# Expert weights by chunk, a hinted branch and an earlier read of z in a two-layer MoE backbone

## The chip, the cores and the metric

The kernel runs on one core of a Trainium2 chip. The metric is the device time of one execution in microseconds; each kernel is run several times, and the median is given. A trace of one more execution comes from the hardware profiler. Engines are named as the profile names them: PE (TensorE), PEld (its weight loads), DVE (VectorE), ACT (ScalarE), POOL (GpSimd) and SP (SyncE, which here only issues DMAs). A trailing q (PEq, SPq) is an engine's sequencer.

## What is computed

Two layers work on 256 latent and 256 context tokens of width 1024, all float32. Layer 0 has an even mixer (a short gated convolution beside differential attention), layer 1 an odd one (a bidirectional gated linear recurrence, RG-LRU). Each layer ends in a mixture of 16 experts, in 4 groups of 4; each token picks its best group and the two best experts in it. The change concerns these two mixtures:

```python
def hier_moe(h, w_grp, b_grp, w_rt, b_rt, w_gate, w_up, w_down):
    ...
    top_v, top_i = lax.top_k(e_sel, TOP_K)
    w_sel = jax.nn.softmax(top_v, axis=-1) * p_sel
    eid = g_idx[..., None] * EXPERTS_PER_GROUP + top_i
    gate = jnp.sum(jax.nn.one_hot(eid, N_EXPERTS, dtype=f32) * w_sel[..., None], axis=-2)
    hg = jnp.einsum('bsd,edf->bsef', h, w_gate)
    hu = jnp.einsum('bsd,edf->bsef', h, w_up)
    act = jax.nn.silu(hg) * hu * gate[..., None].astype(h.dtype)
    return jnp.einsum('bsef,efd->bsd', act, w_down)
```

`w_gate` and `w_up` are 1024x512 for each expert, `w_down` is 512x1024. Layer 0 works on all 512 tokens, layer 1 on the 256 latent ones.

## The kernel before

**Routed rows in slots.** Each expert has a fixed number of slots: `CAP0` = 96 (three row groups of 32, `NR`) in layer 0, `CAP1` = 64 (two, `NR1`) in layer 1. The experts are worked in four groups q = 0 to 3 of four. `four` (L1059) computes one product for the four experts at once: expert j's 32 rows stand as weights in a strip of 32 columns of the array (`tile_position=(0, 32*j)`), its 512 weight columns stream, and the sum over the contraction runs over chunks of 128: 8 for `wg` and `wu`, 4 for each half of `wd`. One *set* is one chunk of one row group: four products, which the trace shows as eight matmul instructions (float32 goes in two passes) and eight weight loads.

**Weights.** They come in tiles of 128x2048 (1 MB) into a pool of 23 units (`unit`, L94), reused in the order in which they come free. `load_ahead` (L118) issues the next loads of the list `todo` on SP while a unit is free and the number loaded ahead is under a limit; `wtile` takes the next tile, `used` gives it back. A tile of `wg` or `wu` holds one expert's four chunks, so `four` takes four tiles, uses them for all row groups and then frees the four together:

```python
for k0 in range(0, nk, 4):
    ws = [get(j, k0) for j in range(4)]
    for r in range(nr):
        for k in range(4):
            for j in range(4):
                T.matmul(...)
        between(r)
    used(*ws)
```

**A group.** `moe0` (L1082) and `moe1` (L1270) do, for each q: `wg` products, `silu` on ACT, `wu` products, `act` on DVE, the transposes of `act` (`transposed_act`, L1073), then the `wd` products of both halves of the output. In layer 0 the outputs of the first three groups go with indirect DMAs on POOL (`scatter`) to a DRAM tile `z` that has one row for each of a token's two choices; rows of the last group, and of tokens over capacity, are zeroed there by scatters of a zero tile. In layer 1 the outputs are summed on PE by a selection matrix `own` (L1326) into four banks that are held to the end.

**The branch.** A count of spilled rounds, `n`, is read by every engine. `spill_rounds` (L970) opens `tc.If(n > 0)` (L977) around a body for rows over capacity. With these inputs n is 0 in both layers, so the body is jumped over. It stands between the last transposes of group q = 3 and that group's `wd` products. Behind layer 0's branch SP issues the gates, four reads of `z` (1 MB each, `zb`), the first tile of the odd mixer's input projection, and then layer 1's modulation weights (`ada`). POOL sums and gates `zb` (L1221, L1222), DVE builds `own` (L1219) and later adds `zb` to `x` (L1249). In layer 1 half of the last group's `wd` loads stand behind the branch, because four tiles at a time come free.

**The order of work** is set by the order of the code on each engine's queue; every SP load waits for its unit and, at a branch, SP waits until the loads that it has issued have landed.

## Time and profile before

| | before |
|---|---|
| median of 3 runs, us | 1024.35 (1023.33 to 1025.01) |
| the profiled execution, us | 1023.78 |
| its span, us | 1022.0 |
| granted clock of TensorE, mean | 0.969 |
| PE, PEld, DVE, ACT, POOL busy | 93%, 51%, 42%, 28%, 13% |
| read from HBM | 303.23 MB |

Times in the trace count from the start of the span. A row of a timeline gives the start, the duration, the engine, the source line, the operation, the tile written and the tiles read, the number of instructions drawn together, and in brackets the idle time before it with what ended it. Layer 0's mixture of experts lies at about 325 to 619 us, layer 1's at about 788 to 1018 us. [...]

### The profile page before, as it was taken

The numbers are of one execution on the slowest core, as the hardware profiler recorded it, in microseconds if no ns is written. First come the engines' busy times: TensorE is split into PE (matmuls) and PEld (weight loads), VectorE is DVE, ScalarE is ACT, GpSimd is POOL, SyncE is SP. The second block draws the span as 40 slices with busy tenths as digits, with TensorE's granted clock in tenths as the row PEclk, the third lists the DMA queues.
The fourth block names the chain that finished last, engine by engine and source line by source line (L and its number), as shares of the span: only waits on it lengthen the run. The fifth ranks groups of instructions, "written<-read, shape, count | busy, mean of one in ns | idle before, by whom it ended". The sixth has DMA issues, their size and how long they took to land. (4 is left out here: it accounts for less than half of the span.)

```text
span 1022.0 us, 16136 instructions
## 1 busy us (share of the span) xinstructions
PE 946.8 (93%) x6705; PEld 516.2 (51%) x6705; DVE 424.2 (42%) x929; ACT 285.0 (28%) x503; POOL 137.7 (13%) x116
## 2 busy tenths in 40 slices
PE   4699999999995999999999799998986999999997
PEld 2488757656885343343433245787634443434333
DVE  3756766567465020020110157858866221212103
ACT  3623333324031110010110025669873110101000
POOL 0254010031033011011010161130410000000000
PEclk9799999999995999999999899999998999999999
DMA  8932466879667799999999787406585499999995
GB/s 363 381 110 114 165 211 252 323 267 420 262 211 274 294 391 404 421 410 416 421 361 422 260 319 284 165 1 211 181 321 214 165 421 420 421 420 420 422 382 203
DMA packets 49201, 309.68 MB, mean 303 GB/s; under 512 B 7432, under 2 KB 8200, under 8 KB 14560
## 3 DMA queue, kind: packets, MB, share of 16 engines
q1 hardware_dynamic: 45296, 300.58, 74.0%
q0 software_dynamic: 3824, 7.99, 2.1%
q8 instruction: 55, 0.90, 0.4%
q14 instruction: 26, 0.21, 0.1%
HBM read 303.23 MB, written 9.50 MB: 306 GB/s over the span
## 5 line engine op out<-in xcount | busy, mean ns | idle before, releaser
L1067 PE MATMUL ba<-w,hgT 128*32 128x512 f32 x1536 | 179.8, 593 | 1.0 <-DMA w<-in_wu_dram 0.9
L1067 PEld LDWEIGHTS ba<-w,hgT 128*32 128x32 f32 x1536 | 54.3, 110 | 114.1 <-issue 110.0
L1067 PE MATMUL ba<-w,actT 128*32 128x512 f32 x800 | 95.2, 593 | 1.9 <-DVEq L977 1.1
L178 PE MATMUL bz<-hT,wsp 128*128 128x256 f32 (+1 forms) x224 | 77.0, 345 | 0.3 <-ACT hT L155 0.3
L180 PE MATMUL bz<-hT,wsp 128*128 128x256 f32 (+1 forms) x224 | 74.2, 333 | 0.0
L179 PE MATMUL bz<-hT,wsp 128*128 128x256 f32 (+1 forms) x224 | 74.1, 332 | 0.0
L1067 PE MATMUL bz<-w,actT 128*32 128x512 f32 x480 | 56.7, 612 | 7.1 <-PEq L977 7.1
L1067 PEld LDWEIGHTS ba<-w,actT 128*32 128x32 f32 x800 | 33.4, 110 | 56.4 <-issue 49.7
L1067 PE MATMUL bz<-w,hgT 128*32 128x512 f32 x512 | 58.0, 592 | 0.0
L155 ACT ACTIVATE wsp<-w 128x512 fp32r<-128x512 f32 (+1 forms) x60 | 42.7, 765 | 50.0 <-PE bz L180 18.0
L158 DVE TENSOR_TENSOR wsp<-w,wsp 128x512 fp32r<-128x512 f32 (+1 forms) x49 | 48.2, 1013 | 10.2 <-ACT wsp L155 10.2
L178 PEld LDWEIGHTS bz<-hT,wsp 128*128 128x128 f32 x224 | 42.3, 189 | 7.3 <-ACT wsp L155 2.8
L180 PEld LDWEIGHTS bz<-hT,wsp 128*128 128x128 f32 x224 | 42.1, 189 | 4.8 <-issue 0.8
L179 PEld LDWEIGHTS bz<-hT,wsp 128*128 128x128 f32 x224 | 42.3, 189 | 4.3 <-DVE hT L158 0.8
L388 PE MATMUL bz<-w,sT 128*32 128x512 f32 x320 | 38.2, 595 | 4.3 <-DMA w<-in_ada_w_dram 4.3
L179 PE MATMUL bz<-wsp,hT 128*128 128x512 f32 x96 | 39.0, 406 | 3.4 <-DVE wsp L158 3.4
L178 PE MATMUL bz<-wsp,hT 128*128 128x512 f32 x96 | 38.5, 408 | 2.4 <-ACT hT L155 2.4
L1067 PEld LDWEIGHTS bz<-w,actT 128*32 128x32 f32 x480 | 16.6, 113 | 43.7 <-issue 43.7
L180 PE MATMUL bz<-wsp,hT 128*128 128x512 f32 x96 | 38.6, 403 | 0.0
L1452 DVE SCALAR_TENSOR_TENSOR uc<-bz,ocw,uc 128x510 f32<-128x510 f32 (+2 forms) x48 | 35.1, 744 | 8.3 <-ACT uc L1450 7.6
L1467 POOL TENSOR_TENSOR uc<-uc,ii 128x512 f32<-128x512 f32 x16 | 25.8, 1621 | 92.7 <-ACT ii L1421 92.6
L1191 DVE SCALAR_TENSOR_TENSOR act<-ba,tg,silu 128x512 f32<-128x512 f32 x6 | 4.5, 751 | 78.4 <-PE ba L1067 78.4
(374 smaller groups left out, 1465.6 us busy)
## 6 DMA issues: line engine op xcount, KB each, us to landing
w<-in_wg_dram SPq DMA_DIRECT2D x64, 1024.0 KB, 12.3
w<-in_wu_dram SPq DMA_DIRECT2D x64, 1024.0 KB, 12.7
w<-in_wd_dram SPq DMA_DIRECT2D x64, 1024.0 KB, 12.2
w<-in_ada_w_dram SPq DMA_DIRECT2D x48, 1024.0 KB, 8.2
w<-in_od_w_in_dram SPq DMA_DIRECT2D x8, 1024.0 KB, 8.4
w<-in_w_qkv_dram SPq DMA_DIRECT2D x6, 1024.0 KB, 9.2
w<-in_w_conv_dram SPq DMA_DIRECT2D x6, 1024.0 KB, 5.0
w<-in_ev_w_out_dram SPq DMA_DIRECT2D x4, 1024.0 KB, 9.4
```

Source lines behind the costliest of these rows:

```text
L155: S.activation(hi, src, AF.Copy)
L158: (eng or lo_engine()).tensor_sub(lo, src, hi.bitcast(F))
L178: T.matmul(o, l[0], r[0], start=start, stop=False)
L179: T.matmul(o, l[0], r[1], start=False, stop=False)
L180: final[0] = T.matmul(o, l[1], r[0], start=False, stop=stop)
L388: T.matmul(m[32 * j:32 * j + 32], sT[:, k], w[:, j * 512:(j + 1) * 512], start=(k == 0), stop=(k == KD - 1), tile_position=(0, 32 * j))
L1067: T.matmul(o[r][32 * j:32 * j + 32], rows(r, k0 + k)[:, 32 * j:32 * j + 32], ws[j][:, k], start=(k0 + k == 0), stop=(k0 + k == nk - 1), ti ...
L1191: V.scalar_tensor_tensor(act[r], u[r], tg[:, n:n + 1], sl[r], op0=ALU.mult, op1=ALU.mult)
L1452: V.scalar_tensor_tensor(c[:, :, j:256], src[:, :, 0:256 - j], tap, c[:, :, j:256], op0=ALU.mult, op1=ALU.add)
L1467: G.tensor_mul(uc[:, n], uc[:, n], ii)
```

## The change

- **Weights by chunk.** The host lays the expert weights out so that a 1 MB tile holds one chunk of all four experts of a group (`fours`, `w_group`). `four` goes through the chunks one by one, all row groups for each, and frees a tile after its chunk. With `last=4` (the `wu` of layer 0, and both halves of `wd` of its last group) the last four chunks are taken together, row group by row group, as before.
- **A hint for the branch.** `spill_hint(l)` marks, on all five engines, the usual outcome of the branch ahead of the `wu` products of q = 3. The barrier-free form of the branch is asked for.
- **z is cleared once,** in the even mixer: a memset on POOL and four DMAs of 1 MB on SP. The scatters of zeros are gone.
- **z is read ahead of the branch** in layer 0: gates, the four reads, POOL's sums and the first projection tile. DVE's `own` stays behind the branch. The units come from the last `wu` tiles.
- **Layer 1's gates** are read ahead of the branch, and all eight `wd` loads of the last group now stand ahead of it.
- The body of the branch works its 16 experts as four loops of four, so that its code is about four times as long. It is not entered here.

```diff
-    def w_first(l, es):
+    def w_group(l, q):
+
         for n in ("wg", "wu"):
-            for k0 in (0, 4):
-                todo.extend(((n, l, e, k0), [128, 4, 512], a[n][l, e][:, k0:k0 + 4]) for e in es)
-
-    def w_second(l, es):
+            todo.extend(((n, l, q, k), [128, 4, 512], a[n][l, q][:, k]) for k in range(KD))
         for h in range(2):
-            todo.extend((("wd", l, e, h), [128, 4, 512], a["wd"][l, e, h]) for e in es)
+            todo.extend((("wd", l, q, h, k), [128, 4, 512], a["wd"][l, q, h][:, k]) for k in range(4))
...
+    z = dr.tile([2 * NT * 128, D], F, name="z")
+
+    def clear_z():
+
+        zero = piece([128, 512], "zero")
+        G.memset(zero, 0.0)
+        zp = z.rearrange("(p n) (h c) -> p (n h) c", p=128, h=2)
+        for q in range(4):
+            nc.sync.dma_start(zp[:, 4 * q:4 * q + 4], zero[:, None, :].to_broadcast([128, 4, 512]))
...
         kT = headsT(kraw)
+        clear_z()
...
-    def spill_rounds(l, cap, nb, load, key, w, nri, empty=lambda zeros: None, ab=None):
+    def spill_hint(l):
+
+        tc.no_sync_barrier()
+        tc.mark_branch_hint_location(f"spill{l}", "LikelyTaken", engines=tuple(
+            getattr(mybir.EngineType, e) for e in ("PE", "Activation", "DVE", "Pool", "SP")))
+
+    def spill_rounds(l, cap, nb, load, key, w, nri, gates, ab=None):
 
         n = nc.values_load(nri[0:1, 0:1], min_val=0, max_val=4, skip_runtime_bounds_check_because="a sum of four compares")
 
         def keep(*ws):
             pass
 
-        with tc.If(n > 0):
+        tc.no_sync_barrier()
+        with tc.If(n > 0, label=f"spill{l}"):
...
-            gates = gate_rows(l, 5, nb // 2)
             buf = unit([128, 4, 512], "buf")
...
-            empty(y)
...
-                with tc.For_i(0, NE, 1) as e:
+                def expert(q, j):
...
+                for q in range(4):
+                    with tc.For_i(0, 4, 1) as j:
+                        expert(q, j)
...
-    def four(place, nr, rows, nk, get, between=lambda r: None):
+    def four(place, nr, rows, nk, key, last=1, between=lambda r: None):
+
 
         o = [place([128, 512]) for _ in range(nr)]
-        for k0 in range(0, nk, 4):
-            ws = [get(j, k0) for j in range(4)]
+        for ks in [[k] for k in range(nk - last)] + [range(nk - last, nk)]:
+            ws = [wtile((*key, k)) for k in ks]
             for r in range(nr):
-                for k in range(4):
+                for k, w in zip(ks, ws):
                     for j in range(4):
-                        T.matmul(o[r][32 * j:32 * j + 32], rows(r, k0 + k)[:, 32 * j:32 * j + 32], ws[j][:, k],
-                                 start=(k0 + k == 0), stop=(k0 + k == nk - 1), tile_position=(0, 32 * j))
-                between(r)
+                        T.matmul(o[r][32 * j:32 * j + 32], rows(r, k)[:, 32 * j:32 * j + 32], w[:, j],
+                                 start=(k == 0), stop=(k == nk - 1), tile_position=(0, 32 * j))
+                if k == nk - 1:
+                    between(r)
...
-        z = dr.tile([2 * NT * 128, D], F, name="z")
         mix3 = unit([128, 2, D], "ys2")
-        zero = mix3[:, 1]
-        G.memset(zero, 0.0)
...
+        def read_z(zs, gates):
+
+            zt = z.rearrange("(i b p) d -> b p i d", i=2, p=128)
+            for b in range(NT):
+                nc.sync.dma_start(zs[b], zt[b])
+            for b in range(NT):
+                G.tensor_add(zs[b][:, 0], zs[b][:, 0], zs[b][:, 1])
+                G.tensor_mul(zs[b][:, 0], zs[b][:, 0], gates[:, b // 2])
...
-        for r in range(NR):
-            scatter(tid[:, NB - NR + r, 1:2], zero)
...
+        load_ahead(15)
...
-            g = four(bank8, NR, lambda r, k: hgT[r][:, k], KD, lambda j, k0: wtile(("wg", 0, 4 * q + j, k0)))
+            g = four(bank8, NR, lambda r, k: hgT[r][:, k], KD, ("wg", 0, q))
             sl = [piece([128, 512], "silu") for _ in range(NR)]
             for r in range(NR):
                 silu[0] = S.activation(sl[r], g[r], AF.Silu)
-            u = four(bank8, NR, lambda r, k: hgT[r][:, k], KD, lambda j, k0: wtile(("wu", 0, 4 * q + j, k0)))
+            if q == 3:
+                spill_hint(0)
+            u = four(bank8, NR, lambda r, k: hgT[r][:, k], KD, ("wu", 0, q), 4)
...
+            else:
+
+                give(hg01, ys01, mix3)
+                gates = gate_rows(0, 5, 2)
+                zs = [unit([128, 2, D], "zb") for _ in range(NT)]
+                read_z(zs, gates)
+                todo.popleft()
+                load_ahead(len(loaded) + 1)
+                ahead[0] = 3
...
-                o = four(bank8, NR, at, 4, lambda j, k0: wtile(("wd", 0, 4 * q + j, h)))
+                o = four(bank8, NR, at, 4, ("wd", 0, q, h))
...
-        give(hg01, hgT01, ys01, mix2, mix3)
-        spill_rounds(0, CAP0, NT, again, key, w, nri, empty)
-        gates = gate_rows(0, 5, 2)
-        zt = z.rearrange("(i b p) d -> b p i d", i=2, p=128)
-        zs = []
-        for b in range(NT):
-            zs.append(unit([128, 2, D], "zb"))
-            nc.sync.dma_start(zs[b], zt[b])
+        give(hgT01, mix2)
+        spill_rounds(0, CAP0, NT, again, key, w, nri, gates)
         own = unit([128, NR, NT, 128], "own", R)
         yl = [unit([128, 2, D], "yl", R) for _ in range(NR)]
-        resume(3)
         for j in range(NR):
             for b in range(NT):
                 V.tensor_scalar(own[:, j, b], slot0, last[:, j, b:b + 1], None, op0=ALU.is_equal)
-        for b in range(NT):
-            G.tensor_add(zs[b][:, 0], zs[b][:, 0], zs[b][:, 1])
-            G.tensor_mul(zs[b][:, 0], zs[b][:, 0], gates[:, b // 2])
...
-        put(0, four(lambda s: bank(s, "z"), NR, at, 4, lambda j, k0: wtile(("wd", 0, 12 + j, 0))))
-        put(1, four(lambda s: bank(s, "z"), NR, at, 4, lambda j, k0: wtile(("wd", 0, 12 + j, 1)), between))
+        put(0, four(lambda s: bank(s, "z"), NR, at, 4, ("wd", 0, 3, 0), 4))
+        put(1, four(lambda s: bank(s, "z"), NR, at, 4, ("wd", 0, 3, 1), 4, between))
...
+        load_ahead(18)
...
-            u = four(bank, NR1, rows, KD, lambda j, k0: wtile(("wu", 1, 4 * q + j, k0)))
+            if q == 3:
+                spill_hint(1)
+            u = four(bank, NR1, rows, KD, ("wu", 1, q))
...
-                spill_rounds(1, CAP1, nb, whole, key, w, nri, ab=ab)
+                spill_rounds(1, CAP1, nb, whole, key, w, nri, gates, ab=ab)
...
+    def fours(w):
+
+        return np.moveaxis(w.reshape(2, 4, 4, *w.shape[2:]), 2, -2)
...
-        "wg": kp(i["moe_w_gate"]), "wu": kp(i["moe_w_up"]), "wd": halves(i["moe_w_down"]),
+        "wg": fours(kp(i["moe_w_gate"])), "wu": fours(kp(i["moe_w_up"])), "wd": fours(halves(i["moe_w_down"])),
```

SP's queue around layer 0's branch, first before, then with the change. `wd` are the last group's output weights, `zb<-z` the reads of z, `od_w_in` the odd mixer's projection, `ada_w` the modulation weights; the rows of the body are left out between COMPARE_AND_BRANCH and UNCONDITIONAL_BRANCH.

```order
L125 DMA w<-in_wu_dram 128x2048 x8
L125 DMA w<-in_wd_dram 128x2048 x7
L972 TENSOR_LOAD nri_2511
L977 COMPARE_AND_BRANCH
...
L977 UNCONDITIONAL_BRANCH x2
L125 DMA w<-in_wd_dram 128x2048
L434 DMA gates<-rows_1747 128x1024 x2
L1213 DMA zb<-z 128x2x1024 x4
L125 DMA w<-in_od_w_in_dram 128x2048
L125 DMA w<-in_ada_w_dram 128x2048 x8
```

```order
L125 DMA w<-in_wd_dram 128x2048 x7
L1738 BRANCH_PREFETCH_HINT
L125 DMA w<-in_wd_dram 128x2048
L425 DMA gates<-rows_1754 128x1024 x2
L1121 DMA zb<-z 128x2x1024 x4
L125 DMA w<-in_od_w_in_dram 128x2048
L973 TENSOR_LOAD nri_2518
L979 COMPARE_AND_BRANCH
...
L979 UNCONDITIONAL_BRANCH x2
L125 DMA w<-in_ada_w_dram 128x2048 x8
```

The last `wd` load, the gates, the four reads of z and the projection's tile have moved ahead of the branch; the modulation weights stay behind it.

SP's queue around layer 1's branch, before and with the change (`out_dram<-xx` are the stores of the result):

```order
L125 DMA w<-in_wu_dram 128x2048 x8
L125 DMA w<-in_wd_dram 128x2048 x4
L972 TENSOR_LOAD nri_2511
L977 COMPARE_AND_BRANCH
...
L977 UNCONDITIONAL_BRANCH x2
L125 DMA w<-in_wd_dram 128x2048 x4
L434 DMA gates<-rows_1163 128x1024
```

```order
L125 DMA w<-in_wd_dram 128x2048 x8
L1738 BRANCH_PREFETCH_HINT
L425 DMA gates<-rows_1170 128x1024
L973 TENSOR_LOAD nri_2518
L979 COMPARE_AND_BRANCH
...
L979 UNCONDITIONAL_BRANCH x2
L1375 DMA out_dram<-xx 128x512 x4
```

The last four `wd` loads and the gates have moved from behind the branch to ahead of it.

PE's queue in layer 0 at the step from the `wg` to the `wu` products of the last group, before and with the change (`ba` and `bz` are banks of PSUM, `hgT` and `hg` the transposed rows of the three row groups):

```order
L1067 MATMUL ba_69<-w,hgT 32x512 x16
L1067 MATMUL bz_63<-w,hgT 32x512 x16
L1067 MATMUL ba_70<-w,hg_2427 32x512 x16
L1067 MATMUL bz_64<-w,hgT 32x512 x16
L1067 MATMUL ba_67<-w,hgT 32x512 x16
L1067 MATMUL bz_65<-w,hg_2427 32x512 x16
```

```order
L1072 MATMUL ba_69<-w,hgT 32x512 x4
L1072 MATMUL bz_63<-w,hgT 32x512 x4
L1072 MATMUL ba_70<-w,hg_2434 32x512 x4
L1738 BRANCH_PREFETCH_HINT
L1072 MATMUL bz_64<-w,hgT 32x512 x4
L1072 MATMUL ba_67<-w,hgT 32x512 x4
L1072 MATMUL bz_65<-w,hg_2434 32x512 x4
```

Sixteen products of one row group (four chunks) have become four (one chunk), the row groups alternate, and the hint stands ahead of the first `wu` product.

## Rows read from the trace of the kernel before

**Rows 1.** The page's busy times of the engines over the span.

```profile
PE 946.8 (93%) x6705; PEld 516.2 (51%) x6705; DVE 424.2 (42%) x929; ACT 285.0 (28%) x503; POOL 137.7 (13%) x116
```

**Rows 2.** Instructions of the branch's line, both layers: ns min/median/max, first and last start.

```profile
L977 PEldq COMPARE_BRANCH  x2: 409/3860/7312, 575.6 to 993.7; - x2
```

**Rows 3.** Timeline of PE, first products behind layer 0's branch.

```profile
583.05 16.02 PE L1067 MATMUL bz<-w,actT 128*32 128x512 f32 x126 [7.07 <-PEq L977]
```

**Rows 4.** Windows: length, busy PE PEld DVE ACT POOL, granted clock, DMA share, GB/s.

```profile
95.00:106.00 11.00, 11.00 (x49) 8.87 (x48) 10.65 (x40) 5.19 (x10) 1.98 (x2) 1.00 0.00 0
576.00:583.00 7.00, 0.00 (x0) 0.00 (x0) 0.00 (x0) 0.00 (x0) 0.00 (x0) 0.82 0.93 324
583.00:588.00 5.00, 4.95 (x28) 1.41 (x32) 0.00 (x0) 0.00 (x0) 4.56 (x2) 0.57 1.02 410
...
806.00:990.00 184.00, 181.86 (x1514) 72.78 (x1506) 29.92 (x69) 20.10 (x35) 0.00 (x0) 1.00 1.01 417
990.00:995.00 5.00, 3.58 (x20) 1.30 (x13) 1.44 (x2) 0.60 (x1) 0.00 (x0) 1.00 0.68 243
```

**Rows 5.** Timeline of SP behind layer 0's branch.

```profile
574.66 2.58 SPq L1213 DMA_DIRECT2D zb<-z  x4
...
583.53 29.15 SPq L125 DMA_DIRECT2D w<-in_ada_w_dram  x8
```

**Rows 6.** Timelines of POOL and DVE: sums of z, their reader, and `own`.

```profile
583.36 2.35 POOL L1221 TENSOR_TENSOR zb<-zb 128x1024 f32<-128x1024 f32 x1 [49.20 <-DMA zb<-z]
...
600.12 2.41 POOL L1222 TENSOR_TENSOR zb<-zb,gates 128x1024 f32<-128x1024 f32 x1
...
542.50 2.44 DVE L1219 TENSOR_SCALAR own<-slot,last 128x128 fp32r<-128x128 f32 x12 [13.00 <-DMA z<-ys,tid]
...
589.45 0.69 DVE L890 TENSOR_TENSOR yl<-bz,yl 128x512 fp32r<-128x512 f32 x1 [13.75 <-ACT yl L889]
...
603.61 1.21 DVE L1249 TENSOR_TENSOR xx<-xx,zb 128x1024 f32<-128x1024 f32 x1
```

**Rows 7.** Timeline of PE, first products with layer 1's modulation weights.

```profile
618.16 2.78 PE L388 MATMUL ba<-w,sT 128*32 128x512 f32 x24
```

**Rows 8.** Timeline of PE in layer 1: groups 0, 1, 2 and 3.

```profile
832.65 13.94 PE L1067 MATMUL ba<-w,actT 128*32 128x512 f32 x128 [0.25 <-ACT actT L231]
...
884.29 1.03 PE L1078 MATMUL ba<-ident,act 128*128 128x128 f32 x8
885.58 8.78 PE L1067 MATMUL ba<-w,actT 128*32 128x512 f32 x72 [0.25 <-ACT actT L231]
...
920.12 2.15 PE L1297 MATMUL ba<-S,hp 128*128 128x256 f32 x16
...
939.35 8.78 PE L1067 MATMUL ba<-w,actT 128*32 128x512 f32 x72 [0.25 <-ACT actT L231]
...
992.26 0.65 PE L1078 MATMUL ba<-ident,act 128*128 128x128 f32 x4
...
995.00 8.78 PE L1067 MATMUL ba<-w,actT 128*32 128x512 f32 x72 [1.10 <-DVEq L977]
1003.71 2.13 PE L1326 MATMUL bz<-ys,own 128*128 128x512 f32 x8
...
1013.83 2.21 PE L1326 MATMUL bz<-ys,own 128*128 128x512 f32 x8
```

**Rows 9.** Layer 1: SP's first issue after the loads ahead; PE's weight loads, last group.

```profile
806.10 8.00 SPq L125 DMA_DIRECT2D w<-in_wd_dram  x6
...
985.28 0.16 PEld L1067 LDWEIGHTS ba<-w,hgT 128*32 128x32 f32 x8 [1.48 <-DMA w<-in_wu_dram]
```

**Rows 10.** First mixer: the page's DMA issues (KB each, us to landing); SP; PE.

```profile
h2d<-h SPq DMA_DIRECT2D x4, 512.0 KB, 3.0
...
109.79 35.41 SPq L125 DMA_DIRECT2D w<-in_ada_w_dram  x8
...
139.05 1.04 PE L388 MATMUL bz<-w,sT 128*32 128x512 f32 x2
```

More of the change, by code (lines that the diff above doesn't have):

```diff
@@ L126, in load_ahead @@
             loaded.append((key, w))
-    def resume(n):
-        assert todo.popleft() is None
-        load_ahead(n)
     def wtile(key):
@@ L309, in backbone @@
     for q in range(4):
-        w_first(0, range(4 * q, 4 * q + 4))
-        w_second(0, range(4 * q, 4 * q + 4))
+        w_group(0, q)
     todo.append(None)
@@ L322, in backbone @@
     for q in range(4):
-        w_first(1, range(4 * q, 4 * q + 4))
-        w_second(1, range(4 * q, 4 * q + 4))
+        w_group(1, q)
     load_x(0)
@@ L935, in down @@
             put(h, slots_by(actT, [s[h] for s in srcs], 4, done))
-    def wget(n, l, e):
-        return lambda k0: wtile((n, l, e, k0))
-    def dget(l, e):
-        return [lambda k0, h=h: wtile(("wd", l, e, h)) for h in range(2)]
     def slots_of(key, w, nb, target, off):
@@ L989, in spill_rounds @@
             with tc.For_i(0, n, 1):
-                with tc.For_i(0, NE, 1) as e:
+                def expert(q, j):
                     def dyn(src):
                         def get(k0):
-                            nc.sync.dma_start(buf, src.rearrange("o p k f -> (o p) k f")[:, k0:k0 + 4])
+                            nc.sync.dma_start(buf, src[:, k0:k0 + 4, bass.ds(j, 1)].rearrange("p k o f -> p k (o f)"))
                             return buf
@@ L999, in spill_rounds @@
                         V.tensor_scalar(hgT[:, k], hgT[:, k], ab[0][k], ab[1][k], op0=ALU.mult, op1=ALU.add)
-                    t = act_of(*[slots_by(hgT, [dyn(a[m][l, bass.ds(e, 1)])], KD, keep) for m in ("wg", "wu")])
-                    down(t, lambda h, o: evict(y[:, h * 512:(h + 1) * 512], o), [[dyn(a["wd"][l, bass.ds(e, 1), h]) for h in range(2)]], keep)
+                    t = act_of(*[slots_by(hgT, [dyn(a[m][l, q])], KD, keep) for m in ("wg", "wu")])
+                    down(t, lambda h, o: evict(y[:, h * 512:(h + 1) * 512], o), [[dyn(a["wd"][l, q, h]) for h in range(2)]], keep)
                     SwT = transposed(hgT[:, 0:nb], Sw.rearrange("p b n -> p (b n)"), nb)
@@ L1012, in spill_rounds @@
             spare.clear()
-            give(gates, buf, hy, *places, *more)
+            give(buf, hy, *places, *more)
     def slot_rows(nb, nr, goh, ef, pos, w):
@@ L1112, in scatter @@
             puts.append(st)
-        def empty(zeros):
-            row = small([128, 2, NT], "row")
-            V.tensor_scalar(row, pos, float(CAP0), float(BIG), op0=ALU.is_lt, op1=ALU.mult)
-            V.tensor_add(row, row, fld[:, :, :, 1])
-            rowi = small([128, 2, NT], "rowi", I32)
-            V.tensor_scalar(rowi, row, float(BIG), None, op0=ALU.add)
-            for i in range(2):
-                for b in range(NT):
-                    scatter(rowi[:, i, b:b + 1], zeros)
+        def read_z(zs, gates):
[5 more added lines that the diff above has]
+                G.tensor_mul(zs[b][:, 0], zs[b][:, 0], gates[:, b // 2])
         def again():
@@ L1219, in moe0 @@
                 V.tensor_scalar(own[:, j, b], slot0, last[:, j, b:b + 1], None, op0=ALU.is_equal)
-        for b in range(NT):
-            G.tensor_add(zs[b][:, 0], zs[b][:, 0], zs[b][:, 1])
-            G.tensor_mul(zs[b][:, 0], zs[b][:, 0], gates[:, b // 2])
         sq = small([128, NT, 2], "sq_sums")
@@ L1330, in moe1 @@
         for q in range(4):
-            g = four(bank, NR1, rows, KD, lambda j, k0: wtile(("wg", 1, 4 * q + j, k0)))
+            g = four(bank, NR1, rows, KD, ("wg", 1, q))
             later()
@@ L1355, in moe1 @@
             for h in range(2):
-                o[h] = four(bank, NR1, at, 4, lambda j, k0: wtile(("wd", 1, 4 * q + j, h)))
+                o[h] = four(bank, NR1, at, 4, ("wd", 1, q, h))
                 if h == 0:
```

## The prediction

> **What bounds the kernel now.** I read the page's busy times first, then the branch's line, the timelines of PE and SP around both branches, and the stretches by window. TensorE is busy for 93% of the span [rows 1], so only what makes PE wait, and what PE then repeats at a low clock, is worth time. PE waits in two places that the change touches.
>
> First, the branch of layer 0. The branch's line shows one long sequencer stop of PE, 7312 ns, and one short, 409 ns [rows 2]. The PE timeline puts the long one in layer 0: 7.07 us of idle, released by PE's own sequencer [rows 3]. In 576 to 583 us no engine computes while the DMA engines move 324 GB/s [rows 4]: PE waits for neither data nor another engine, but for its code. In the next 5 us the granted clock is 0.57, so the halt is paid a second time.
>
> Second, the end of layer 1. From 806 to 990 us the DMA engines run full, at 417 GB/s [rows 4], and PE is busy for 181.9 of 184 us: two limits that lie almost on top of each other, and in the last group the loads win (1.48 us of wait for a tile of `wu`, [rows 9]). From 990 to 995 us, around the branch, the rate falls to 243 GB/s: SP stands at its branch until its loads have landed.
>
> The sum is made against the profiled execution, 1023.8 us (span 1022.0), 0.6 under the median of the three runs, 1024.35.
>
> **Branch of layer 0.** The hint names the outcome 24 sets of products ahead (a set is one chunk of one row group, all four experts), so PE's code is there when the branch comes. Gone are 7.07 us of halt and 5.0 x (1 - 0.57) = 2.1 us of half-clock work behind it, 9.2 together; I leave 0.4, what the other branch costs PE [rows 2]. **-8.8.** Its bounds are 0 and -9.2.
>
> What is moved ahead of this branch has to be covered. SP issues gates, four 1 MB reads of `z` and the first tile of layer 1's input projection from units freed by the last `wu` tiles. Four of those tiles are freed together at the end of `wu`, near 573 us, so the last read and the projection's tile start where all four reads stood before (574.66, [rows 5]); at 417 GB/s two of them need 5 us, and SP then leaves the branch at about 579. Its ada loads began at 583.53 and are first used at 618.16 [rows 5, 7], 609 in the new time: 30 us of slack. POOL's eight steps take 600.12 + 2.41 - 583.36 = 19.2 us [rows 6]; with reads from about 561 us on they end near 582, and their first reader on DVE stands at 603.61, 594.8 in the new time: 12 us to spare. Were that cover gone, each late microsecond would cost one. DVE's twelve `own` steps, 2.44 us, fall behind the branch, where DVE has nothing to do for 13.75 us, until ACT hands it the first output products [rows 6]: hidden. **0**, upper bound +2.4.
>
> **Chunk by chunk, layer 0.** PE shows no wait for weights there, and the number of products is the same. **0**, bounds -1 to +1.
>
> **Chunk by chunk, layer 1.** A set, eight product instructions in the trace, takes 13.94 / 16 = 0.87 us [rows 8]. Before, four tiles come free after eight sets, at 806.1 [rows 9]; now the first comes free after two, six sets or 5.2 us earlier, at 801. From there 78 tiles have to come (96 less the 18 loaded ahead), each 1.0486 MB / 417 GB/s = 2.51 us: the last lands at 801 + 2 + 195.8 = 998.8.
>
> What would PE do if it never waited? From one group's first `wd` product to the next it takes 939.35 - 885.58 = 53.8 us, and 995.00 - 939.35 = 55.65 into the last [rows 8]. The last lacks two gathers of 2.15 us, so 49.5; turning `act` stands uncovered there (2.74 us from first turn to first `wd` product against 1.29), so 50.9. **-4.7**: this is the waits for weights and for the branch. The bounds are 0, if the loads stay late, and -6.2, if the turning also shrinks to 1.3.
>
> In the last group's `wd`, 1013.83 - 995.00 = 18.83 us pass from its first product to the second adds [rows 8]. Less the 2.06 of the first adds, 16.8 us are left for what took 13.94 in the first group: all eight `wd` tiles are now asked for before the branch, and no longer half of them behind it. **-2.8**, bounds 0 and -2.9. The first half's adds now stand behind the last products, and their chain on DVE with them: **+0.3**, bounds 0 to +2.1, the adds' own time.
>
> By these numbers PE wants the last tile at 990.3 + 7 x 1.74 = 1002.5, 3.7 us after it lands; the first `wd` tiles have a lead of the same kind. PE, not the loads, is the limit, by little.
>
> **Clearing z.** Row scatters of zeros go, and 4 MB of zeros are written by SP in the first mixer. SP is past its loads there, and the DMA engines move nothing from 95 to 106 us [rows 4]. At 417 GB/s the 4 MB take 10 us; by the four 0.5 MB stores of `h`, 3.0 us each [rows 10], 8 x 3.0 = 24. Either way they end by 119; the ada loads behind them on SP start at 109.79 and are first used at 139.05. **0**, bounds 0 to +2. The POOL memset stands where POOL has little to do. What is saved at the head of layer 0's experts lies beside PE work: 0, bounds -1 to 0.
>
> **Sum:** 1023.8 - 8.8 - 4.7 - 2.8 + 0.3 = 1007.8, said as **1008.0**. With the bounds that are near rows (a stall of 0 to 3 us left over, 2 us of loads late at the end of layer 1, clear_z at +2) this case spans 1003 to 1012.
>
> **Rivals.** *The hint does not hold.* It asks for code 24 sets of products and some turns ahead, and whatever PE fetches for its own line in between may push it out; then the change does not do what it says at the branches. Layer 0's halt would be between the 0.4 and the 7.3 us of [rows 2]; with one read and one load in flight in place of four reads I take 3.4. Layer 1 paid only 0.4 with empty queues; now eight loads are queued there and the skipped body is four times as long, so I take 8.5: 7.3 and a part of its low clock. 1007.8 + 11.9 = 1020 (1014 to 1025). For it: 24 sets with their weight loads are 24 x 16 = 384 instructions of PE between hint and branch. Against it: PE is never seen to stop for its straight-line code in 184 us of full DMA queues [rows 4]. Chance 0.22.
>
> [...]
>
> *Only the branch gains.* Loads in layer 1 stay as late as before, since a unit freed earlier starts a transfer on queues that are already full (417 GB/s in [rows 4]). For it: that rate can't rise. Against it: 5 us of empty queues ahead of 806.1. 1023.8 - 8.8 = 1015. Chance 0.08.
>
> *The hint halts PE itself (slower).* If fetching the hinted code displaces what PE runs next, PE stops at the hint, in mid-stream, for as long as a fetch takes behind full queues: 7.3 us and the 2.1 of low clock, at each of two hints, and again at the branches as in the first rival: 1007.8 + 18.8 + 7.4 = 1034. It decides once the two halts together pass 16 us, the whole gain. Against it: the full queues did not stop PE before [rows 4]. Chance 0.05.
>
> **How the numbers follow.** My forecast has 0.60, these three 0.22, 0.08 and 0.05, and 0.05 is left for more than I found on either side. The range 1003 to 1020 holds the forecast's own 1003 to 1012, the second rival and the lower half of the first: about 0.8. A measurement of this kernel tells some 2 us, 0.2%, from no change. Faster by more: 0.60 + 0.22 + 0.08, **0.90**; the same: **0.05**, from the first rival's top and part of the rest; slower: **0.05**, the third.
>
> **What would show it.** Right: PE's stop at the layer-0 branch under 1 us and a clock of 1.0 after it; DMA at full rate from about 801 us of the old time to the end of layer 1's loads, with no dip at the branch; the last group's `wd` products in one stretch of about 14 us; POOL's sums over before DVE asks. Wrong: a sequencer stop at either branch above 3 us; PE waits for `wu` or `wd` tiles in the last group; a PE halt at a hint; a wait for ada loads near 139 us.

## The result, and the profile after

The changed kernel takes 1010.28 us (median of 4 runs, 1008.83 to 1011.24) beside 1024.23 for the one before; the ratio is 0.9861 with a 95% interval of 0.9849 to 0.9873. Forecast were 1008.0 us and a range of 1003 to 1020. The sign, the size and the range were right; the way to it was not, as the stages show. The profiled execution took 1010.48 us, its span is 1008.7.

| the same step in both traces | before, us | after, us | after is ahead by |
|---|---|---|---|
| first set of layer 0's experts | 333.88 | 335.10 | -1.2 |
| last transposes ahead of layer 0's branch | 573.30 | 574.52 | -1.2 |
| first product behind that branch | 583.05 | 576.82 | 6.2 |
| first product with layer 1's modulation weights | 618.16 | 610.78 | 7.4 |
| layer 1's experts, first product | 797.82 | 788.54 | 9.3 |
| first `wd` product of group 0 | 832.65 | 823.30 | 9.4 |
| of group 1 | 885.58 | 874.19 | 11.4 |
| of group 2 | 939.35 | 926.54 | 12.8 |
| of group 3, behind layer 1's branch | 995.00 | 982.90 | 12.1 |
| end of the span | 1022.0 | 1008.7 | 13.3 |

Of the first 1.2 us, 0.9 are there at 35 us already, before anything that the change touches.

PE passes both branches. The instructions of the branch's line (ns min/median/max, first and last start) answer to [rows 2]:

```profile
L979 PEldq COMPARE_BRANCH  x2: 350/364/379, 576.1 to 976.6; - x2
L979 ACTq COMPARE_BRANCH  x2: 49/58/68, 576.2 to 976.3; - x2
L979 PEldq EVENT_SEMAPHORE  x2: 51/51/51, 576.6 to 977.0; - x2
L979 ACTq EVENT_SEMAPHORE  x2: 17/17/17, 576.7 to 981.8; - x2
L979 DVEq COMPARE_BRANCH  x2: 74/79/84, 576.9 to 977.3; - x2
L979 DVEq EVENT_SEMAPHORE  x2: 21/21/21, 581.5 to 982.8; - x2
L979 POOLq COMPARE_BRANCH  x2: 54/63/72, 587.3 to 780.3; - x2
L979 POOLq EVENT_SEMAPHORE  x2: 17/17/17, 592.7 to 780.7; - x2
```

PE's 7312 ns have become at most 379. But read the two lines of each engine together: on DVE, ACT and POOL the branch itself is over in 0.1 us, and the semaphore instruction that comes next on the skipping path starts later. On DVE that gap is 4.6 us in layer 0 and 5.5 in layer 1, on ACT 5.5 in layer 1, on POOL 5.4 in layer 0. In the kernel before, DVE's gap was 0.6 us at both branches:

```profile
L977 DVEq COMPARE_BRANCH  x2: 62/67/72, 575.6 to 994.3; - x2
L977 DVEq EVENT_SEMAPHORE  x2: 21/21/21, 576.2 to 994.9; - x2
```

So the halt has gone from PE to others. Packets of the instruction queues, 81 in the whole span of the kernel before, come in each of these gaps: three (two of 8 KB, one of 16) in PE's of the kernel before, between 578 and 580.5 us, and with the change five in DVE's of layer 0, four in DVE's and ACT's of layer 1 and two in POOL's.

What that costs is seen in PE's timeline around layer 1's branch, which answers to [rows 8]:

```profile
823.30 13.94 PE L1072 MATMUL ba<-w,actT 128*32 128x512 f32 x128 [0.25 <-ACT actT L226]
...
970.79 1.92 PE L1072 MATMUL ba<-w,hgT 128*32 128x512 f32 x16 [0.55 <-DMA w<-in_wu_dram]
973.27 1.92 PE L1072 MATMUL ba<-w,hgT 128*32 128x512 f32 x16 [0.56 <-DMA w<-in_wu_dram]
...
982.90 16.27 PE L1072 MATMUL ba<-w,actT 128*32 128x512 f32 x128 [6.11 <-DVEq L979]
999.10 3.95 PE L1326 MATMUL bz<-ys,own 128*128 128x512 f32 x16
```

Its last row but one: 6.11 us of idle, released by DVE's sequencer at the branch, and then 16.27 us for products that take 13.94 in the first group. Some 1.1 us of the idle time was there before ([rows 8]); the rest is DVE's halt. The windows (columns as in [rows 4]) give the reason for the second number, a granted clock of 0.53 over 5.1 us, where it is 1.00 from 795 to 970 us, behind a stretch of 12.90 us in which PE is busy for 5.40:

```profile
795.00:970.00 175.00, 174.22 (x1506) 64.06 (x1494) 28.05 (x64) 19.96 (x35) 0.00 (x0) 1.00 1.01 419
970.00:982.90 12.90, 5.40 (x44) 1.70 (x41) 2.39 (x5) 0.60 (x1) 0.00 (x0) 0.92 1.01 415
982.90:988.00 5.10, 5.10 (x28) 1.46 (x32) 0.67 (x3) 0.00 (x0) 0.00 (x0) 0.53 1.01 411
```

And DVE's timeline behind layer 0's branch, then POOL's around it, which answer to [rows 6]:

```profile
581.64 8.86 DVE L1221 TENSOR_SCALAR own<-slot,last 128x128 fp32r<-128x128 f32 x12 [4.72 <-DVEq L979]
```

```profile
569.86 2.37 POOL L1123 TENSOR_TENSOR zb<-zb 128x1024 f32<-128x1024 f32 x1 [33.71 <-DMA zb<-z]
...
586.78 2.46 POOL L1124 TENSOR_TENSOR zb<-zb,gates 128x1024 f32<-128x1024 f32 x1
```

The twelve `own` steps took 2.44 us before and take 8.86 now, from 581.64 to 590.5, beside POOL's sums, which run from 569.86 to 589.2. They have also changed sides: before, they began at 542.50 ([rows 6]), 33 us ahead of DVE's branch, though the code of both kernels has them behind it.

### The profile page after: what moved, and what is told of

Same layout as the page of the kernel before. It is cut to its first block, busy times and chain, and to the rows that moved or that the text cites. A ratio compares the mean times of both kernels' runs of the same rounds, so it can differ in the third digit from the quotient of the medians.

```text
span 1008.7 us, 16130 instructions
## 1 busy us (share of the span) xinstructions
PE 938.0 (93%) x6705; PEld 507.0 (50%) x6705; DVE 429.0 (43%) x929; ACT 285.2 (28%) x503; POOL 135.4 (13%) x113
## 5 line engine op out<-in xcount | busy, mean ns | idle before, releaser
L1072 PEld LDWEIGHTS ba<-w,hgT 128*32 128x32 f32 x1536 | 49.4, 110 | 112.1 <-issue 105.9
L1072 PE MATMUL bz<-w,hgT 128*32 128x512 f32 x512 | 64.8, 592 | 0.0
L1072 PEld LDWEIGHTS ba<-w,actT 128*32 128x32 f32 x800 | 26.5, 112 | 64.9 <-issue 60.2
L153 DVE TENSOR_TENSOR wsp<-w,wsp 128x512 fp32r<-128x512 f32 (+1 forms) x49 | 46.8, 983 | 10.7 <-ACT wsp L150 10.7
L1342 DVE SCALAR_TENSOR_TENSOR act<-ba,tg,silu 128x512 f32<-128x512 f32 x8 | 6.0, 748 | 88.1 <-PE ba L1072 88.0
L1192 DVE SCALAR_TENSOR_TENSOR act<-bz,tg,silu 128x512 f32<-128x512 f32 x6 | 4.5, 751 | 79.9 <-PE bz L1072 79.9
L1192 DVE SCALAR_TENSOR_TENSOR act<-ba,tg,silu 128x512 f32<-128x512 f32 x6 | 4.5, 750 | 78.3 <-PE ba L1072 78.3
```

Source lines behind the costliest of these rows:

```text
L153: (eng or lo_engine()).tensor_sub(lo, src, hi.bitcast(F))
L1072: T.matmul(o[r][32 * j:32 * j + 32], rows(r, k)[:, 32 * j:32 * j + 32], w[:, j], start=(k == 0), stop=(k == nk - 1), tile_position=(0, 32 ...
L1192: V.scalar_tensor_tensor(act[r], u[r], tg[:, n:n + 1], sl[r], op0=ALU.mult, op1=ALU.mult)
L1342: V.scalar_tensor_tensor(act[r], u[r], tg[:, n:n + 1], sl[r], op0=ALU.mult, op1=ALU.mult)
```

## The experiments

All are built on the changed kernel; medians of before were 1024.2 to 1025.4 beside them.

### The length of the skipped body

`e1_rolled_body`:

```diff
-                for q in range(4):
+                with tc.For_i(0, 4, 1) as q:
                     with tc.For_i(0, 4, 1) as j:
                         expert(q, j)
```

(with the weights' address taken from both loop registers).

> The changed kernel, but the body of the branch is written once, in a loop over four groups of four experts, in place of four copies. Theory A (the length of the skipped body decides): in the changed kernel DVE stands 4.6 us at layer 0's branch and 5.5 us at layer 1's, because the code behind the longer body is no longer at hand and the hint does not bring it there; with the short body DVE passes each branch within 1 us, as before, PE's 6.1 us wait in layer 1 falls to about 1, and the 2.3 us of low clock behind it go: 1010 - 5 - 2.3 = about 1003. Theory B (the queue decides: a fetch stands behind eight weight loads, however long the body is): DVE's halt in layer 1 stays near 5 us and the time near 1010.

Measured: 1010.3 us (ratio 0.9847, 0.9829 to 0.9865). The trace bears out theory A and the time does not. The gaps are gone:

```profile
L979 DVEq COMPARE_BRANCH  x2: 74/79/84, 576.3 to 981.3; - x2
L979 DVEq EVENT_SEMAPHORE  x2: 21/21/21, 576.9 to 981.9; - x2
L979 POOLq COMPARE_BRANCH  x2: 54/61/68, 585.9 to 783.8; - x2
L979 POOLq EVENT_SEMAPHORE  x2: 17/17/17, 587.8 to 784.2; - x2
```

DVE passes each branch in 0.6 us. The queues are as full as ever, which rules theory B out: all eight `wd` loads are issued ahead of layer 1's branch here too (958.83 to 977.65), and PE waits for the last of them as late as 997.13 us (0.56 us). What was won in layer 1 (4.2 us from the first `wd` product of group 0 to the last adds) was lost in layer 0, on DVE and PE (4.8 us from the last transposes to the first modulation product, 41.10 in place of 36.26); first the instructions of the tile `own` (ns min/median/max, first and last start), then PE's timeline:

```profile
L1221 DVE TENSOR_SCALAR own<-slot,last x12: 274/1302/2431, 577.0 to 590.6; 128x128 fp32r<-128x128 f32 x12
```

```profile
593.98 8.33 PE L1232 MATMUL ba<-yl,own 128*128 128x512 f32 x23 [3.39 <-DVE yl L892]
602.24 7.07 PE L1072 MATMUL bz<-w,actT 128*32 128x512 f32 x64
```

`own` again: one step takes 274 ns at best and 2431 at worst, as long as one of POOL's sums (2.37). DVE is free 4.6 us earlier, starts `own` in the midst of the sums (they end at 587.8, and POOL has additions of its own from 588.0 on), is through with it at 591.9, and the `yl` that PE waits for stands behind it: 3.39 us, and then 8.33 us for what takes 5.8, at a clock of 0.62 (a window from 593.98 to 602).

### The hint

`e2_no_hint` and, with the short body, `e3_rolled_no_hint`:

```diff
-            if q == 3:
-                spill_hint(0)
...
-            if q == 3:
-                spill_hint(1)
```

> The changed kernel without either hint. If the hint is what frees PE in layer 0: PE halts there again for 5 to 8 us and works 4 to 5 us at half clock behind it, so that layer 0 gives back 7 to 10 us. In layer 1 PE would halt beside DVE, for about the same 5 to 8 us, so little is added there: 1017 to 1022 in all. If the hint does nothing and the earlier read of z alone made PE's halt go, the time stays at 1010.

Measured: 1015.5 (0.9909, 0.9892 to 0.9925), 5.2 us over the changed kernel and below the 1017 to 1022 that I expected. PE halts at both branches:

```profile
L979 PEldq COMPARE_BRANCH  x2: 5123/5715/6307, 575.9 to 978.5; - x2
...
L979 DVEq COMPARE_BRANCH  x2: 63/68/72, 576.6 to 979.3; - x2
L979 DVEq EVENT_SEMAPHORE  x2: 21/21/21, 580.7 to 984.9; - x2
```

5.1 us in layer 0, 6.3 in layer 1, where DVE halts beside it for 5.6: as expected, the second costs little more than DVE's alone. So the hint frees PE. For DVE it does nothing: 4.1 and 5.6 us without it, 4.6 and 5.5 with it. Less is lost than expected: PE's halt in layer 0 is at the low end of 5 to 8 us, the slower products behind it cost 1.3 (15.23 us for 13.94), and the halt also hides the slow `own` (8.78 us here).

> Short body and no hint, the branch as it was before, with all else changed. Theory A: layer 0's PE halt is back (7 us and 2 of low clock, since PE's body was out of reach before as well), layer 1 has none on PE or DVE: 1003 + 9 = about 1012. Theory B: halts in both layers, 1018 or more.

Measured: 1011.1 (0.986, 0.9844 to 0.9877). Theory A's 1012, and only 0.8 us over `e1_rolled_body`: PE halts 5.3 us in layer 0 and passes layer 1's branch in 0.4. So the hint seemed to be worth nothing. It was worth as much as the collision of `own` with the sums, since PE's halt hides the one or pays for the other.

### Out of POOL's way

`e5_own_ahead` (short body):

```diff
+            if q == 3:
+                give(hg01)
+                own = unit([128, NR, NT, 128], "own", R)
+                for j in range(NR):
+                    for b in range(NT):
+                        V.tensor_scalar(own[:, j, b], slot0, last[:, j, b:b + 1], None, op0=ALU.is_equal)
             g = four(bank8, NR, lambda r, k: hgT[r][:, k], KD, ("wg", 0, q))
```

and the same lines taken out behind the branch.

> Short body as in e1_rolled_body, and DVE's twelve own steps moved ahead of the last group's wg products, so that they are over before POOL begins to sum z. Theory (DVE and POOL get in each other's way): own took 14.95 us beside POOL's sums in e1_rolled_body, 8.86 in the changed kernel and 2.44 alone in the kernel before; ahead of the sums it takes 2.4 to 3 again, PE's wait of 3.4 us for yl and the 2.5 us of low clock behind it go, and the time falls from 1010.3 to about 1004.5. Rival: the steps are slow for another reason (the clock, the loads that land meanwhile); then they stay at 9 us or more and the time at 1010.

Measured: 1004.06 us (0.9803, 0.9785 to 0.9821), as expected. PE's timeline behind layer 0's branch has no wait and no slow stretch left:

```profile
577.11 13.94 PE L1072 MATMUL bz<-w,actT 128*32 128x512 f32 x128 [0.64 <-ACTq L979]
590.98 5.82 PE L1234 MATMUL ba<-yl,own 128*128 128x512 f32 x24
596.74 7.07 PE L1072 MATMUL bz<-w,actT 128*32 128x512 f32 x64
```

`own` takes 2.25 us, from 534 to 537. This is about where the kernel before had it. The rival, a slow step for want of clock or beside the loads, falls by the other traces as well: in the kernel before, `own` took 2.44 us while the DMA engines moved 430 GB/s, and in the changed kernel 8.86 us at a granted clock of 1.00, beside 350 GB/s. And not every step of DVE is slowed. An addition that has one of its inputs from a bank of PE's output (PSUM) keeps its 0.69 us beside a sum of POOL's (583.63 to 586.02):

```profile
584.92 0.69 DVE L892 TENSOR_TENSOR yl<-bz,yl 128x512 fp32r<-128x512 f32 x1 [2.79 <-ACT yl L891]
```

> The changed kernel with its long body, and own ahead as in e5_own_ahead. DVE still halts 4.7 and 5.5 us at the branches. Layer 0 gets back only the 0.8 us that PE loses there now; layer 1's halt stays: 1009 to 1010. Against e5_own_ahead it prices the long body once own is out of the way: 4 to 5 us.

`e6_own_ahead_long_body` has the same edit with the long body. Measured: 1010.1 (0.986, 0.9843 to 0.9876). So the four copies of a body that is never entered cost 6.0 us, where 4 to 5 were expected: 5.3 from layer 1's first `wd` product to its last adds (180.21 us in place of 174.88; PE waits 6.41 us for DVE's sequencer there) and 0.7 in layer 0 (35.41 in place of 34.72).

> As e5_own_ahead, without hints. In e3_rolled_no_hint the hint seemed worth 0.8 us, since PE's halt hid own. With own out of the way it shows its whole price: PE's halt of 5.3 us and 2.8 us of low clock come back, 1004.5 + 8 = 1012 to 1013. If the hint is worth little in itself, 1005 to 1006.

`e7_own_ahead_no_hint`: 1010.5 (0.9867, 0.9850 to 0.9883), 6.4 us over `e5_own_ahead`; 8 was expected. PE halts 5.1 us and takes 1.7 us longer for the products behind it (15.63 us for 13.94). The hint's price is that, and the 0.8 of before was not.

`e8_z_read_late`, `read_z` and the first projection load put behind `spill_rounds`:

```diff
...
-                zs = [unit([128, 2, D], "zb") for _ in range(NT)]
-                read_z(zs, gates)
...
         spill_rounds(0, CAP0, NT, again, key, w, nri, gates)
...
+        zs = [unit([128, 2, D], "zb") for _ in range(NT)]
+        read_z(zs, gates)
...
```

> As e5_own_ahead, but z is read and summed behind the branch, as before. By the prediction's cover: four reads from about 575 us take 10 us, POOL's sums run 580 to 599, DVE wants the first at 592 and the last near 602, the modulation loads start 5 to 8 us later and have 30 us of slack: 0 to 2 us slower than e5_own_ahead. If the early read is what the change needs, 5 us or more slower.

Measured: 1013.0 (0.989, 0.9873 to 0.9906), 8.9 us over `e5_own_ahead`, where I expected 0 to 2. The sums end at 601.4, when DVE has begun to add them to `x` (DVE's timeline, then POOL's, then PE's):

```profile
596.36 2.82 DVE L1250 TENSOR_TENSOR xx<-xx,zb 128x1024 f32<-128x1024 f32 x1
599.10 2.86 DVE L543 TENSOR_TENSOR xx<-xx,gy 128x512 f32<-128x512 f32 x1
```

```profile
598.17 3.24 POOL L1124 TENSOR_TENSOR zb<-zb,gates 128x1024 f32<-128x1024 f32 x1
```

```profile
610.13 0.79 PE L1234 MATMUL ba<-yl,own 128*128 128x512 f32 x1 [5.01 <-ACT yl L891]
```

An addition of 1.21 us in [rows 6] takes 2.82 and one of 0.69 takes 2.86, and POOL's last two sums take 2.88 and 3.24 us; ACT's squares wait for DVE's additions, the `yl` behind the squares too, and PE waits 5.01 us. To these come 0.78 us at one more wait, 2.0 in the products behind the waits (7.07 us for 21 of them, where 24 take 5.79) and 1.2 in the first products behind the branch (15.10 for 13.94). In the kernel before, PE's halt covered all this. Once the hint has taken the halt away, the early read is what the gain rests on.

### Layer 1

`e4_four_at_a_time`:

```diff
-        for ks in [[k] for k in range(nk - last)] + [range(nk - last, nk)]:
+        for ks in [range(k, k + 4) for k in range(0, nk, 4)]:
```

> The changed kernel, but four chunk tiles are taken together and freed together everywhere, row group by row group, as the order of products was before. It tells what the finer release is worth in layer 1. By the prediction the loads of layer 1 start 5 us later, PE waits for tiles in the last group and half of its wd loads stand behind the branch: up to 7 us slower than the changed kernel, 1014 to 1017. If the finer release gives nothing (the rival in which only the branch gains), 1010.

Measured: 1019.2 (0.9943, 0.9926 to 0.996): 9 us worse than the changed kernel, where I expected 4 to 7. SP's first load stands at 799.58, in the changed kernel at 792.51; layer 1 itself begins 4.5 us later (first `wd` product at 827.79), so about 2.6 of the 7.1 are release. PE waits four times for `wu` in the last group:

```profile
966.56 1.06 PE L1072 MATMUL ba<-w,hgT 128*32 128x512 f32 x8 [0.33 <-DMA w<-in_wu_dram]
969.05 6.22 PE L1072 MATMUL ba<-w,hgT 128*32 128x512 f32 x56 [1.42 <-DMA w<-in_wu_dram]
976.52 1.07 PE L1072 MATMUL ba<-w,hgT 128*32 128x512 f32 x8 [1.26 <-DMA w<-in_wu_dram]
979.01 6.00 PE L1072 MATMUL ba<-w,hgT 128*32 128x512 f32 x40 [1.42 <-DMA w<-in_wu_dram]
```

4.4 us of waits, 1.1 in the changed kernel. From group 0's first `wd` product to the last adds it is 184.3 us in place of 179.75: about half of the 9 us. The other half is layer 0, 41.3 us in place of 36.3 from the last transposes to the first modulation product. The finer release also starts the reads of `z` sooner (POOL's sums begin at 572.90 here, 569.86 in the changed kernel); with the later sums `own` takes 11.39 us, PE waits 3.52 for `yl` and then takes 8.11 for what takes 5.8.

`e9_four_loads_fewer`: the second half of the last group's `wd` is not loaded, and the tiles of the first half are used twice. So half of that group's output is worked out from other weights: this measures the loads, and is no version of the kernel.

> As e5_own_ahead, but the second half of the last group's output weights in layer 1 is not loaded: the tiles of the first half are used for both halves, so that 4 of 96 tiles of 1 MB are left out there and the result's second half is computed from other weights. Theory (in layer 1 the loads, not PE, set the end once DVE's halt is gone): the waits for wd tiles between the last products, 0.2 + 0.65 + 0.47 + 0.57 + 0.55 = 2.4 us, go, and the time falls from 1004 to 1001 to 1002. If PE is the limit, as the prediction had it, those waits have another cause and the time stays at 1004.

Measured: 1000.8 us (0.9765, 0.9749 to 0.9782), 3.2 under `e5_own_ahead`. The waits between the last products are gone; first `e5_own_ahead`, then this kernel:

```profile
974.33 5.36 PE L1072 MATMUL ba<-w,actT 128*32 128x512 f32 x48 [1.18 <-DVEq L979]
979.88 1.92 PE L1072 MATMUL ba<-w,actT 128*32 128x512 f32 x16 [0.20 <-DMA w<-in_wd_dram]
982.46 1.92 PE L1072 MATMUL ba<-w,actT 128*32 128x512 f32 x16 [0.65 <-DVE ys L892]
984.85 1.92 PE L1072 MATMUL ba<-w,actT 128*32 128x512 f32 x16 [0.47 <-SPq L979]
987.34 1.92 PE L1072 MATMUL ba<-w,actT 128*32 128x512 f32 x16 [0.57 <-SPq L979]
989.81 1.92 PE L1072 MATMUL ba<-w,actT 128*32 128x512 f32 x16 [0.55 <-DMA w<-in_wd_dram]
```

```profile
975.23 14.29 PE L1076 MATMUL ba<-w,actT 128*32 128x512 f32 x128 [1.18 <-DVEq L979]
989.45 3.98 PE L1333 MATMUL bz<-ys,own 128*128 128x512 f32 x16
```

One tile every 2.4 to 2.5 us in the first, the pace of the loads (eight in 19.86 us, from 871.56 to 891.42); three rows name DVE or SP and not a tile, but the tiles that SP's branch waits for, until 987.5 us, are the same. Once the halts are gone, the loads set layer 1's end.

### Hint on PE alone, and the clear

`e10_hint_on_pe_long_body` and `e11_hint_on_pe_short_body`:

```diff
-            getattr(mybir.EngineType, e) for e in ("PE", "Activation", "DVE", "Pool", "SP")))
+            getattr(mybir.EngineType, e) for e in ("PE",)))
```

> As e6_own_ahead_long_body (long body, own ahead), with the hint on PE alone. In e2_no_hint, with the same long body, ACT passed both branches within 0.5 us and POOL halted 1.9 us in layer 0; with hints on all engines ACT halts 5.5 us in layer 1 and POOL 5.4 us in layer 0. Theory: the hints on ACT and POOL do harm, and those two halts go back to 0.5 and 1.9 us here, while DVE halts 4 to 6 us at both branches either way. The time hangs on DVE in layer 1 and stays near 1010. Rival: the halts of ACT and POOL have to do with what the other engines fetch at that moment; then they stay at 5 us.

Measured: 1011.05 us in one run. The theory fell: ACT, with no hint of its own, still halts in layer 1 (976.6 to 982.4) and POOL in layer 0 (587.3 to 592.1). Why neither halted so long in `e2_no_hint`, with the same body, stays open.

> As e5_own_ahead (short body, own ahead), with the hint on PE alone. No other engine halts with the short body, hint or not, so the time is that of e5_own_ahead, 1003 to 1005.

Measured: 1003.3 us (0.9791, 0.9775 to 0.9808), with `e5_own_ahead` (1004.06, not told apart) the fastest version with the whole computation; with the short body the other engines need no hint: ACT, DVE and POOL pass both branches in 0.4 to 1.9 us here.

`e12_clear_twice` is `e11_hint_on_pe_short_body` with the stores of zeros issued twice.

> As e11_hint_on_pe_short_body, but the four stores that clear z are issued twice, 8 MB in place of 4. If the clear is free where it stands (the prediction's 0), the second pass is free too or nearly so: it takes 10 to 24 us more of SP and the DMA engines from about 110 us on, and the modulation weights are wanted at 140: 1003 to 1005. If the clear costs something already, its price doubles here and shows as PE waiting for modulation weights near 140 us: 2 us or more, 1005 to 1010.

Measured: 1004.65 (0.98, 0.9784 to 0.9816), not told apart from 1003.3. SP is held 13.1 us by the eight stores in place of 3.5, and PE's first modulation product stands at 139.15, where it was before at 139.05. The clear is free where it stands.

## Why the prediction was right, and where it was not

- **The halt, -8.8: right.** From the last transposes to the first modulation product, layer 0 takes 36.3 us in place of 44.9: -8.6. The clock stays at 1.0 behind the branch (13.87 us for 128 product instructions, before 15.95). `e7_own_ahead_no_hint` prices the hint at 6.4 with z read early, less than the 9.2 of before: PE halts 5.1 us there, before 7.07. Why it halts for less is not shown.
- **The rival in which the hint does not hold** was wrong for PE, of which it spoke; a like halt came on DVE, hint or not. I looked for the halt on PE, as it had been there, and passed over that the body is four times as long on every engine. DVE's gaps are 4.6 and 5.5 us over the long body and 0.6 over the short one (`e1_rolled_body`); PE's hinted branch takes 0.4 us over either. That PE waited "for its code" fits the three instruction packets in its halt; that it waited for just these is not shown. That code asked for ahead of time can be pushed out, or can push out what PE runs next, as this rival and the third had it, was a guess that no run shows. The hint stands 33 to 44 us ahead of DVE's branch and 20 to 25 ahead of PE's; whether the lead matters was not tested.
- **`own`, 0, "hidden": wrong.** DVE had 13.75 us with nothing to do; the step that failed is that it could work in them at its own speed. 2.44 us became 8.86, and 14.95 in `e1_rolled_body`, where PE paid 5.9 us. Beside the sums one step of DVE can take as long as a whole instruction of POOL: one of `own` takes 274 to 2431 ns in `e1_rolled_body`, where the sums take 2.36 to 2.45 us each, and the additions in `e8_z_read_late` agree (2.82 and 2.86 us, beside sums of 2.88 and 3.24). Why the two engines hold each other up is shown by no run. The forecast's own times had `own` beside the sums: they were to run to 582, and DVE without a halt starts it at 577 (`e1_rolled_body`). What that costs was not asked. Nor was it seen that the trace had `own` ahead of the branch before, where it met no sums: the change itself put the two side by side. Why the order of DVE's queue differs between two kernels whose code has the same order here is shown by no run; that the order of the code sets it does not hold for these steps.
- **The cover of POOL's sums, 12 us to spare: 6.1, and enough.** The first read is issued about when forecast (561), and so is the first reader (594.8); SP's timeline, then DVE's:

```profile
559.20 13.23 SPq L1121 DMA_DIRECT2D zb<-z  x4
```

```profile
595.33 1.71 DVE L1248 TENSOR_TENSOR xx<-xx,zb 128x1024 f32<-128x1024 f32 x1
```

  But the sums end at 589.2, not near 582. They begin 10.7 us after the first issue, where the forecast left about 2 and [rows 5, 6] had 8.7 (574.66 to 583.36). By the forecast's time they would just have been over at 581.64, when DVE begins `own` in this kernel, so the mis-sized read is a part of that miss too. And I costed the early read at nothing and did not see that it was needed: late, it costs 8.9 us.
- **Layer 1, -4.7 up to the last `wd` products: wrong on both sides.** From group 0's first `wd` product to group 3's it is 159.6 us in place of 162.35, so -2.8; with the halt away (`e5_own_ahead`) 153.6, -8.8. The step that failed is "what would PE do if it never waited": I took 53.8 us for an undisturbed group. The windows of groups 0 to 1 and 1 to 2, before and then after, show the same work in less:

```profile
832.65:885.58 52.93, 52.68 (x441) 20.10 (x441) 10.18 (x26) 6.22 (x12) 0.00 (x0) 1.00 1.01 420
885.58:939.35 53.77, 53.30 (x440) 23.11 (x440) 10.09 (x25) 6.33 (x12) 0.00 (x0) 1.00 1.01 421
```

```profile
823.30:874.19 50.89, 50.64 (x441) 19.73 (x441) 10.15 (x26) 6.22 (x12) 0.00 (x0) 1.00 1.01 421
874.19:926.54 52.35, 52.09 (x440) 19.47 (x441) 10.01 (x25) 6.22 (x12) 0.00 (x0) 1.00 1.01 420
```

  2.0 and 1.4 us less, at the same clock, the same number of instructions and no wait. Before, the order of PE's instructions broke sets in two (13 products of a row group here, 3 there, with gathers between); the weight loads before show such a piece, three in a step of 0.43 us that takes four:

```profile
870.54 0.13 PEld L1067 LDWEIGHTS ba<-w,hgT 128*32 128x32 f32 x4 [0.30 <-issue]
870.97 0.12 PEld L1067 LDWEIGHTS ba<-w,hgT 128*32 128x32 f32 x3 [0.30 <-issue]
871.40 0.12 PEld L1067 LDWEIGHTS ba<-w,hgT 128*32 128x32 f32 x3 [0.31 <-issue]
```

  With the change the sets stay whole in these groups; `e4_four_at_a_time`, whose sets are whole too, also takes 50.9 from group 0 to group 1 and waits for weights later. In every run with the new layout these two groups take 50.9 to 51.0 and 52.3 to 52.7 us. So the finer release is not the reason; that the broken sets are is read from these rows and runs, and no run changed the order alone.
- **The last `wd` products, -2.8 and +0.3: not in this kernel.** From the first of them to the last adds it is 20.15 us, before 21.04, so -0.9, low clock and all. It is 18.2, the -2.8 of the sum, only in `e9_four_loads_fewer`. "PE, not the loads, is the limit, by little" failed: PE wants its tiles 3.7 us sooner than I had it, by the whole sets (in `e9_four_loads_fewer` it is 153.99 us from group 0's first `wd` product to group 3's, 157.65 by the forecast), and the last of 78 loads is there 199.8 us behind the first issue in `e5_own_ahead` (from 789.93 to about 989.8, where PE's last wait for a tile ends) in place of 197.8.
- **Not seen: -1.9 us between the layers** (179.7 to 177.8 from the first modulation product to layer 1's first set). PE's order now has 28 of these products in one piece where it had 12 and waited for DVE behind them; this could be read from the order ahead of time. That it is the reason was not tested, and the stretch takes 176.0 to 178.0 us in the runs with the change, so a part of the 1.9 can be scatter.
- **The clear, 0, and the head of layer 0, 0: right** (`e12_clear_twice`; 0.3 us at the first set).

So -8.6, -1.9, -2.8 and -1.2 behind layer 1's branch, with +1.2 at the start, make the 13.3. Of the signs that the prediction named, those of being right came (PE's stop of 0.4 us, a clock of 1.0 behind it, no dip of the DMA engines at layer 1's branch, 415 and 411 GB/s) and two of being wrong came as well (a halt above 3 us, on DVE, and waits for `wu` in the last group, 0.55 and 0.56 us). That 1008.0 lies so near to 1010.28 is in part luck: two misses of opposite sign, DVE's halt and the whole sets, almost cancel.

## What to carry to other kernels

When a halt goes, list what ran under it on every engine, not only on the one that halted: here DVE's additions against POOL's sums stood ready to take its place. Then see in the trace, and not in the code, what the change itself put side by side: here `own` and the sums, and a longer body with an engine that jumps it. Look at each engine's own rows for what a hint does: here it took PE's stops from 5.1 and 6.3 us to at most 0.38, while DVE's gaps of 4.1 and 5.6 stayed at 4.6 and 5.5. A branch body that is never entered has its price as well, 6.0 us here for four copies in place of one (`e6_own_ahead_long_body`), paid by the engines that jump it, so keep it rolled. And before a stretch is called free of waits, compare its time with that of the same instructions elsewhere: here steps of 0.43 us held three weight loads in place of four, and PE's busy time, 52.68 of 52.93 us, showed nothing of it.

## What was not expected of the hardware

- DVE's compare-against-a-column step on 128x128 takes 0.28 us alone (281 to 287 ns in the kernel before) and up to 2.43 beside POOL's additions, which keep their 2.36 to 2.49 us (changed kernel and `e1_rolled_body`). Beside DVE's own additions of two tiles, in `e8_z_read_late`, POOL is slowed too (2.88 and 3.24 us). An addition with one input from PSUM was not slowed (0.69 us in `e5_own_ahead`).
- A jump over a body takes 0.5 to 1.0 us on DVE with the short body and 3.8 to 5.8 us with four copies of it, with a hint as without one, while PE, which without a hint stood 4.8 to 7.3 us at layer 0's branch in every run, passed both branches in 0.35 to 0.48 with one (given 20 to 25 us ahead in the changed kernel). Why the hint works on PE and not on DVE was not settled.
- Idle time of 3.4 to 7.1 us on PE, at the branches and behind the waits shown here, was followed, each time, by products that took 1.3 to 2.8 us longer than the same products elsewhere. The granted clock of such a stretch was 0.57 in the kernel before (583 to 588 us), 0.53 in the changed kernel (982.9 to 988) and 0.62 in `e1_rolled_body` (593.98 to 602).
